# Three depthwise-conv tiles recast as half-length filters summed by accumulating transfers, and later weight remainders moved to VectorE

## The chip, the cores and the metric

The kernel runs on one core of one Trainium2 chip. The metric is device time of the whole program in microseconds (us), as the median of several runs. Five engines work beside each other: TensorE (PE, matmuls), VectorE (DVE), ScalarE (ACT), GpSimd (POOL) and SyncE (SP, which here only issues transfers). Each of them takes its instructions strictly in the order of the program and waits at the head of its queue for whatever that instruction needs.

## What is computed

One decoder layer over 1024 tokens with 1024 channels. The part that matters here is the conv group, 1024 channels in 8 tiles of 128, with a causal depthwise convolution of 31 taps:

```python
u = h @ w_in[l]
cv, cg, cs, lx, ls = jnp.split(u, [D_CONV, 2*D_CONV, 3*D_CONV, 3*D_CONV + D_LRU], axis=-1)
v = cv * jax.nn.sigmoid(cg)
v = causal_depthwise_conv(v, dw_w[l], dw_b[l])          # 31 taps
v = jax.nn.silu(layernorm(v, cln_g[l], cln_b[l]))       # over all 1024 channels
v = v @ pw2_w[l] + pw2_b[l]
y_conv = v * jax.nn.silu(cs)
...                                                     # lru group: short conv, two gates, linear scan
y = jnp.concatenate([y_conv, y_lru], axis=-1) @ w_out[l]
x = x + (1.0 + gate[:, None, :]) * y
```

An RMSNorm with a modulation computed from `c` comes before, another RMSNorm after.

## The kernel before

**Layout.** Channels lie on the 128 partitions, tokens along the free dimension; one activation tile is 128x1024 f32. There are 47 such buffers in SBUF (`big`). PSUM holds three 128x1024 tiles (`mm`) and one more (`acc`). Every f32 matmul is made of three products of rounded parts: high x high, high x low, low x high. So each weight tile is loaded by SP (`raw`), rounded on ACT (`whi`, L416) and its remainder is taken by a subtraction (`wlo`, `SUB`, L417). `weights()` (L427) does this for one tile; its default engine for the remainder is POOL. `raw`, `whi` and `wlo` have two buffers each.

**Slots.** PE's work goes in slots of 48 matmuls: 4 input tiles first (`FIRST`), 2 (`NEXT`), then the other input tiles mixed with the 8 pairs of lru gates, then 8 tiles of the lru half of the output, then the pointwise matmul and the rest of the output in pairs. `number[s]` numbers the weight tiles in that order: `NEXT` has 4 and 5.

**Order.** `Plan` is a list scheduler that runs at build time. Each operation has an engine, an estimated cost and a priority; `order()` plays them against a clock, takes the ready operation of smallest priority number on each free engine, and writes the program in that order. Conv work has priority number 1000 and up (L887), which fills what the other work leaves; the slots' own work has their number. `lock` marks operations that the planner keeps from running beside each other on DVE and POOL. The order is fixed once built: if an operation comes later on the chip than planned, all behind it on its engine comes later.

**The conv, `conv_tile(i)` (L886).** Six tiles go on DVE. The values are stored with the even tokens in the left half and the odd ones in the right (`apart`/`by_two`, L864 to L868; written by L974 and L1078). With `ev` and `od` those halves, three filters of half length are run over 512 tokens each: the even taps over `ev`, the summed taps over `ev+od`, the odd taps over `od`; 15 + 15 + 14 fused multiply-adds (L924, L926, L931) on accumulators in the PSUM tile `acc`, and three additions or subtractions put the result together. Tiles 2 and 5 (`POOLED`, L46) are done instead as 31 full-length products on ACT (`cq`, L894, L898), added one by one on POOL (L900).

**Around it.** `conv_sum()` (L940) sums the eight tiles in the order `SUMS` (L53), on POOL but for the last. `layer_norm()` (L1037) needs that sum; its mean and its 1/std are spread over the partitions by PE into `acc` tiles (L1039, L1054). `gate_mod()` (L1028) takes the modulation's gate in 8 pieces, one in each slot from `GM` = 22: a product on POOL and its sum on ACT (L715, L716). `gw_load()` (L949) takes the remainders of the gate weights on POOL.

Of the kernel before, what the change touches and what calls it, by code (L numbers as in the profile page):

```python
# [9 lines left out]
F32 = mybir.dt.float32  # L10
# [35 lines left out]
POOLED = (2, 5)  # L46
# [6 lines left out]
SUMS = (0, 1, 3, 2, 4, 6, 5, 7)  # L53
QRES = 4
GM = 22
# [22 lines left out]
class Op:  # L78
    __slots__ = ("eng", "cost", "emit", "prio", "table", "bufs", "succ", "wait", "ready",
                 "seq", "reserve", "columns", "lock", "end", "psum")  # L80


class Plan:
# [7 lines left out]
    def __init__(self, pools):  # L91
        self.pools = pools
        self.ops, self.writer, self.readers = [], {}, {}
# [13 lines left out]
    def op(self, eng, cost, emit, prio, r=(), w=(), table=None, after=(), reserve=0,  # L107
           columns=0, lock=False):
        o = Op()
        o.eng, o.cost, o.emit, o.prio, o.table = eng, cost, emit, prio, table  # L110
        o.succ, o.ready, o.seq, o.reserve = [], 0.0, len(self.ops), reserve
        o.columns = columns
        o.lock = eng == "POOL" or eng == "DVE" and lock
# [24 lines left out]

    def order(self):
# [19 lines left out]
        def done(o, end):  # L159
            o.end = until[o.eng] = end  # L160
            for b, w in o.psum:
                (b.written if w else b.read)[o.eng] = end
            for b in o.bufs:
                b.left -= 1
                if b.left == 0 and b.pool in free:
                    heapq.heappush(releases, (end, b.name, b.pool))
            for s in o.succ:
                lat = 0.0 if o.eng == "PE" and s.eng == "PE" else \
                    0.11 if o.eng == s.eng == "DVE" else self.LATENCY[o.eng]
                s.ready = max(s.ready, end + lat)  # L170
                s.wait -= 1
                if s.wait == 0:
                    pending[s.eng].append(s)

        while left:
# [3 lines left out]
            for e in engines:  # L179
# [42 lines left out]
                if e == "POOL" and held["DVE"] > t + 1e-9:  # L222
                    waiting, until[e] = o, float("inf")
                    continue
# [24 lines left out]
def hymba_layer(ctx: ExitStack, tc: tile.TileContext, xT, c_row, vecs, mod_w, w_first, w_in,  # L249
# [11 lines left out]
    psacc = ctx.enter_context(tc.tile_pool(name="psacc", bufs=1, space=bass.MemoryType.PSUM))  # L261
# [8 lines left out]
    pools["acc"] = (psacc, "acc", [P, T], 1)  # L270
# [46 lines left out]
    def TT(prio, eng, out, a, b, op, n=T, r=(), w=(), reserve=0, after=()):  # L317
        e = dve if eng == "DVE" else pool
        return S.op(eng, d_cost(n) if eng == "DVE" else p_cost(n),
                    lambda: e.tensor_tensor(out=out(), in0=a(), in1=b(), op=op), prio, r, w,  # L320
                    reserve=reserve, lock=not in_psum(r), after=after)

# [129 lines left out]
    def mm_tile(name, parts=2):  # L452
        return S.buf("mm", name, F32, parts)

    def acc_tile(name, parts=2):
        return S.buf("acc", name, F32, parts)
# [187 lines left out]
    psf = [mm_tile(f"first{n}", 4) for n in range(3)] + [acc_tile("first3", 4)]  # L644
    psb = psf[3]
# [15 lines left out]
    def fw_mm(prio, ps, i, xh, xl, k, cols, after=()):  # L661
        _, wh, wl = fw[k - k % 2]

        def emit():
            for lhs, rhs, last in ((wh, xh, 0), (wh, xl, 0), (wl, xh, 1)):
                for a, b in cols:
                    pe.matmul(ps()[:, a:b], fw_part(lhs, k, i * P, i * P + P)(),  # L667
                              rhs()[:, a:b], start=k == 0 and lhs is wh and rhs is xh,
                              stop=k == KT - 1 and bool(last), skip_group_check=True)
# [90 lines left out]
    st, wk = ctile("st", KT), halves(psb, H, T)  # L760

    def stats(sq, k):
        for b in range(KT):
            pe.matmul(psb()[:, H + b:H + b + 1], sq()[:, b * P:b * P + P], ones[:, 0:1],
                      start=k == 0 and b == 0, stop=k == len(sqs) - 1, skip_group_check=True)

    def spread_mm(a, e):
        for b in range(a // P, e // P):
            o = H + b * P - a
# [4 lines left out]
    ACT(RSP, lambda: st, lambda: psb()[:, H:H + KT], AF.Sqrt, KT, bias=eps_t, scale=1.0 / D,  # L774
        r=wk, w=[("st", 0)])
    S.op("DVE", 0.12, lambda: dve.reciprocal(st, st), RSP, [("st", 0)], [("st", 0)])
    for a, e in START:
        spread = S.op("PE", 0.22 * ((e - a) // P), lambda a=a, e=e: spread_mm(a, e), RSP,
                      [("st", 0)], wk, columns=4 * (e - a))
        ACT(RSP, part(rbc, a, e), part(psb, H, H + e - a), "copy", e - a, r=wk,  # L780
# [104 lines left out]

    def conv_tile(i):  # L886
# [6 lines left out]
        if i in POOLED:  # L893
            ACT(pr, ci, vi, AF.Identity, scale=w(0), bias=vec("dw_b", i), r=[vi, ("V", 1)],  # L894
                w=[ci])
            for s in range(1, TAPS):
                q = big_buf(f"cq{i}_{s}")
                ACT(pr, part(q, s, T), part(vi, 0, T - s), AF.Copy, T - s, scale=w(s), r=[vi],  # L898
                    w=[q], reserve=QRES)
                TT(pr, "POOL", part(ci, s, T), part(ci, s, T), part(q, s, T), ALU.add, T - s,  # L900
                   r=[ci, q], w=[ci])
            c[i] = ci
            return


        acc, b2 = acc_tile(f"cacc{i}"), bias2[:, i:i + 1]
        acc_e, acc_s, src_s = half(acc, 0), half(acc, 1), half(ci, 0)
# [8 lines left out]
        def every(o):  # L916
            return lambda: ci().rearrange("p (m q) -> p q m", q=2)[:, o]
        TT(pr, "DVE", src_s, ev, od, ALU.add, H, r=[vi], w=[(ci, 0)])
        ACT(pr, acc_e, ev, AF.Identity, H, scale=w(0), bias=vec("dw_b", i), r=[vi, ("V", 1)],
            w=[(acc, 0)])  # L920
        ACT(pr, acc_s, src_s, AF.Identity, H, scale=ws(0), bias=b2,
            r=[(ci, 0), ("V", 1), ("wsum", 0)], w=[(acc, 1)])
        for r in range(1, 16):
            STT(pr, cut(acc_e, r, H), cut(ev, 0, H - r), w(2 * r), cut(acc_e, r, H), ALU.mult,  # L924
                ALU.add, H - r, r=[vi, (acc, 0)], w=[(acc, 0)])
            STT(pr, cut(acc_s, r, H), cut(src_s, 0, H - r), ws(r), cut(acc_s, r, H), ALU.mult,  # L926
                ALU.add, H - r, r=[(ci, 0), (acc, 1)], w=[(acc, 1)])
        ACT(pr, every(1), acc_s, "copy", H, r=[(acc, 1)], w=[ci])
        ACT(pr, acc_s, od, AF.Copy, H, scale=w(1), r=[vi], w=[(acc, 1)])
        for r in range(1, 15):  # L930
            STT(pr, cut(acc_s, r, H), cut(od, 0, H - r), w(2 * r + 1), cut(acc_s, r, H), ALU.mult,  # L931
                ALU.add, H - r, r=[vi, (acc, 1)], w=[(acc, 1)])
        ACT(pr, every(0), acc_e, "copy", H, r=[(acc, 0)], w=[ci])
        TT(pr, "DVE", every(1), every(1), acc_e, ALU.subtract, H, r=[ci, (acc, 0)], w=[ci])
        TT(pr, "DVE", every(1), every(1), acc_s, ALU.subtract, H, r=[ci, (acc, 1)], w=[ci])
        TT(pr, "DVE", cut(every(0), 1, H), cut(every(0), 1, H), cut(acc_s, 0, H - 1), ALU.add,
           H - 1, r=[ci, (acc, 1)], w=[ci])
# [23 lines left out]
    def evac_in(m, ps, n, b=None, rb=()):  # L961
# [5 lines left out]
        elif kind == CV:  # L967
            sg = sig.pop(i)
            if i in POOLED:
                v[i] = sg  # L970
                TT(pr, "DVE", sg, ps, sg, ALU.mult, r=[ps, sg], w=[sg])
            else:
                v[i] = big_buf(f"v{i}")
                TT(pr, "DVE", apart(v[i], 0, T), by_two(ps, 0, T), by_two(sg, 0, T), ALU.mult,  # L974
                   r=[ps, sg], w=[v[i]])
# [61 lines left out]
    def layer_norm():  # L1037
        pr = 45
        mean = acc_tile("mean")  # L1039
# [14 lines left out]
        bc = acc_tile("lnbc")  # L1054
# [7 lines left out]
    for i, (s, ps) in enumerate(zip(FIRST, psf)):  # L1062
        j, p, bi = s[1] % KT, EVP + i, bias[:, i:i + 1]
        t = big_buf(f"first_u{i}", parts=4)
        for a, e in START:
# [4 lines left out]
            else:  # L1070
                for k in range(KT):
                    fw_mm(RSP + 60 + 0.1 * k, ps, i, uhs[k], uls[k], k, ((a, e),), after=[spread])
                TT(p, "DVE", part(t, a, e), part(ps, a, e), part(rbc, a, e), ALU.mult, n,
                   r=pk + halves(rbc, a, e), w=tk)
# [230 lines left out]
```

## Time and profile before

| | |
|---|---|
| median of 3 runs | 770.67 us (769.59 to 775.23) |
| profiled execution, its own time | 771.28 us |
| its span, first to last instruction | 769.4 us |
| granted TensorE clock, mean | 0.985 of full speed |
| transfers | 77.84 MB, all issued by SP |

The page gives each engine's busy time as a share of the span. A group of instructions is named by line, engine and `out<-in`; two figures behind the bar are its busy time in total and the mean length of one, and what follows is the time that the engine stood idle before them and who ended it. A row of a table of stretches gives for each engine busy us and the number of instructions, then the granted clock, the DMA share and GB/s. PE's matmuls overlap, so the length of one (some 390 ns) is longer than the distance from one to the next.

### The profile page before, as it was taken

Reading aid. Unit: us, or ns where it says so; the run is one execution under the profiler, and the core shown is the slowest. Engines: PE = TensorE matmul, PEld = TensorE weight load, DVE = VectorE, ACT = ScalarE, POOL = GpSimd, SP = SyncE. Lnnn points to the kernel's source line nnn. Section 1 sums busy time; section 2 is a strip of 40 time slices with the busy share of each in tenths; the row PEclk is TensorE's granted clock in tenths of the full one; section 3 lists DMA queues with packets and bytes.
Section 4 is the critical chain, followed back from the end, with each engine's and each line's share of the span. In section 5 each row is a group of like instructions: output and inputs, shape, how many; then the busy total and the mean of one; then the engine's idle time right before and its main releaser. Section 6 shows DMA issues by size and latency. Waiting matters only on the chain.

```text
span 769.4 us, 8629 instructions
## 1 busy us (share of the span) xinstructions
PE 733.5 (95%) x3288; PEld 606.0 (79%) x3288; DVE 665.6 (87%) x806; ACT 420.3 (55%) x473; POOL 323.1 (42%) x132
## 2 busy tenths in 40 slices
PE   3999899999999997999999998999999999999995
PEld 2888677888888885888888787788888888887885
DVE  7999999789899889999897998995977666999565
ACT  6630926997626477955956565664723223455220
POOL 0030312799899469989999612121220000000000
PEclk9999999999999999899999999999999999999997
DMA  9930221102102312331111012433332621425114
GB/s 329 406 118 32 83 82 35 55 27 83 63 28 83 116 55 83 116 110 56 55 55 55 27 55 81 138 136 111 136 115 96 200 110 40 152 83 177 43 55 164
DMA packets 24954, 77.84 MB, mean 101 GB/s; under 512 B 2768, under 2 KB 6096, under 8 KB 24912
## 3 DMA queue, kind: packets, MB, share of 16 engines
q1 hardware_dynamic: 24912, 77.28, 28.5%
q8 instruction: 26, 0.43, 0.2%
q14 instruction: 16, 0.13, 0.1%
HBM read 64.68 MB, written 12.58 MB: 100 GB/s over the span
## 4 chain that ended last, share of the span: by engine, by line
PE 57%; DVE 29%; ACT 7%; POOL 3%; issue 2%; DMA 1%; SPq 0%; DVEq 0%; ACTq 0%; POOLq 0%
PE ps L438 32%; DVE cacc L312 11%; PE first L667 6%; PE papw L559 5%; PE pbpw L559 4%; PE out L605 3%; ACT cq L301 3%; PE paout L559 2%; DVE r L1020 2%; PE pbout L559 2%; DVE xs L312 1%; DVE xs L320 1%; DVE yl L320 1%; DVE sls L320 1%; POOL c L320 1%
## 5 line engine op out<-in xcount | busy, mean ns | idle before, releaser
L320 POOL TENSOR_TENSOR wlo<-raw,whi 128x1024 fp32r<-128x1024 f32 x44 | 115.1, 2615 | 234.5 <-ACT whi L293 234.5
L438 PE MATMUL ps<-uh,whi 128*128 128x512 f32 x576 | 180.5, 395 | 7.0 <-ACT scs L301 6.6
L438 PE MATMUL ps<-ul,whi 128*128 128x512 f32 x576 | 179.7, 393 | 3.6 <-DVE ul L312 3.6
L438 PE MATMUL ps<-uh,wlo 128*128 128x512 f32 x576 | 179.3, 393 | 1.6 <-POOL wlo L320 1.6
L320 POOL TENSOR_TENSOR c<-c,cq 128x1023 f32<-128x1023 f32 (+29 forms) x60 | 159.8, 2663 | 9.5 <-ACT cq L301 7.0
L312 DVE SCALAR_TENSOR_TENSOR cacc<-v,V,cacc 128x511 f32<-128x511 f32 (+14 forms) x174 | 129.6, 745 | 13.7 <-ACT c L293 6.3
L438 PEld LDWEIGHTS ps<-uh,whi 128*128 128x128 f32 x576 | 109.4, 191 | 31.4 <-ACT scs L301 7.5
L438 PEld LDWEIGHTS ps<-ul,whi 128*128 128x128 f32 x576 | 109.3, 190 | 27.7 <-DVE ul L312 4.7
L438 PEld LDWEIGHTS ps<-uh,wlo 128*128 128x128 f32 x576 | 109.2, 190 | 24.8 <-POOL wlo L320 2.0
L293 ACT CAST whi<-raw 128x1024 fp32r<-128x1024 f32 x48 | 50.3, 1047 | 59.6 <-issue 34.4
L301 ACT ACTIVATE cq<-sig,V 128x1023 f32<-128x1023 f32 (+29 forms) x60 | 63.9, 1128 | 1.6 <-POOL c L320 1.6
L312 DVE SCALAR_TENSOR_TENSOR cacc<-c,wsum,cacc 128x511 f32<-128x511 f32 (+6 forms) x84 | 62.7, 746 | 2.3
L301 ACT ACT_TABLE_LOAD x45 | 57.7, 1283 | 1.6 <-PEq L1297 0.7
L438 PE MATMUL ps<-yh,whi 128*128 128x512 f32 x128 | 39.6, 391 | 0.0
L438 PE MATMUL ps<-yh,wlo 128*128 128x512 f32 x128 | 39.4, 389 | 0.0
L438 PE MATMUL ps<-yl,whi 128*128 128x512 f32 x128 | 39.4, 389 | 0.0
L667 PE MATMUL first<-uh,fhi 128*128 128x512 f32 x64 | 26.7, 416 | 11.1 <-ACT uh L301 11.1
L312 DVE SCALAR_TENSOR_TENSOR xs<-ps,V,xs 128x1023 f32<-128x1023 f32 (+2 forms) x24 | 30.6, 1274 | 2.6 <-ACT xs L301 2.5
L438 PEld LDWEIGHTS ps<-yl,whi 128*128 128x128 f32 x128 | 24.0, 188 | 5.0
L438 PEld LDWEIGHTS ps<-yh,wlo 128*128 128x128 f32 x128 | 24.0, 188 | 5.0
L667 PE MATMUL first<-ul,fhi 128*128 128x512 f32 x64 | 26.3, 411 | 1.7 <-DVE ul L312 1.7
L438 PEld LDWEIGHTS ps<-yh,whi 128*128 128x128 f32 x128 | 23.9, 188 | 4.9
(299 smaller groups left out, 1359.7 us busy)
## 6 DMA issues: line engine op xcount, KB each, us to landing
raw<-in_w_in_dram SPq DMA_DIRECT2D x36, 512.0 KB, 3.3
modw<-in_mod_w_dram SPq DMA_DIRECT2D x24, 512.0 KB, 7.8
raw<-in_w_out_dram SPq DMA_DIRECT2D x12, 512.0 KB, 3.9
scsd<-scs SPq DMA_DIRECT2D x8, 512.0 KB, 2.6
acc<-in_xT_dram SPq DMA_DIRECT2D x8, 512.0 KB, 4.6
accd<-acc SPq DMA_DIRECT2D x8, 512.0 KB, 2.8
rawpw<-in_pw_dram SPq DMA_DIRECT2D x8, 512.0 KB, 3.8
scsr<-scsd SPq DMA_DIRECT2D x8, 512.0 KB, 5.3
```

The source lines that it names most:

```text
L293: act.copy(out(), in_())
L301: act.activation(out=out(), in_=in_(), func=func, **kw)
L312: dve.scalar_tensor_tensor(out=out(), in0=in0(), scalar=scalar, in1=in1(), op0=op0, op1=op1, accum_out=accum)
L320: lambda: e.tensor_tensor(out=out(), in0=a(), in1=b(), op=op), prio, r, w,
L438: pe.matmul(ps()[:, a - off:b - off], k3(lhs)()[:, k, :], rhs[k]()[:, a:b], start=(k == 0 and lhs is wh and rhs is xh and (a - off) % H == 0),
L559: pe.matmul(half(*ps)(), half(*lhs)()[:, j * P:j * P + P], half(*rhs)(), start=start and j == 0 and z == 0, stop=j == KT // 2 - 1 and z == ...
L605: pe.matmul(ps()[:, a - off:e - off], k3(lhs)()[:, k, :], rhs()[:, i * H + a % H:i * H + a % H + e - a], start=k == KORD[0] and lhs is wh ...
L667: pe.matmul(ps()[:, a:b], fw_part(lhs, k, i * P, i * P + P)(), rhs()[:, a:b], start=k == 0 and lhs is wh and rhs is xh, stop=k == KT - 1 a ...
L1020: S.op("DVE", 2.2, lambda: dve.tensor_tensor_scan(out=r(), data0=a(), data1=xs(), initial=0.0, op0=ALU.mult, op1=ALU.add), pr, [a, xs], [r])
```

## The change

It has four parts.

1. `POOLED` becomes (2, 4, 5). These three tiles get the half-length form as well, in `conv_pooled`: ACT makes products of 512 tokens, two of them (even-tap and summed-tap filter) side by side in one 128x1024 buffer, and a transfer issued by POOL adds that buffer to the accumulator `es` in SBUF; pairs of odd-tap products go to `oo` in the same way. 22 such transfers for one tile. Four DVE operations and two ACT copies put the result together. No POOL arithmetic is left in these tiles, and each v is stored apart, as for the other tiles.
2. `weights()` takes the remainder on POOL only for tiles numbered under `EARLY` = 10, later ones on DVE.
3. The PSUM tile `acc` becomes two half tiles of 128x512. The two accumulators of a DVE conv tile are held apart; `first3`, the token statistics and the late half of the fourth first tile get one each; the mean and 1/std of the layer norm go into `mm` tiles.
4. `apart` and `by_two` keep the same places, but walk all even tokens and then all odd ones, instead of pairs. `SUMS` becomes (0, 1, 3, 2, 6, 4, 7, 5). In the DVE conv tiles the copy of `acc_e` and its subtraction come ahead of the odd filter.

The planner's model of an accumulating transfer is: `ISSUE` = 1.0 us on POOL, then landed `FLIGHT` = 7.0 us later, and not less than `RATE` = 3.0 us after the one before.

```diff
-POOLED = (2, 5)
+POOLED = (2, 4, 5)
-SUMS = (0, 1, 3, 2, 4, 6, 5, 7)
+SUMS = (0, 1, 3, 2, 6, 4, 7, 5)
+AHEAD = 3
+FOLD = "DVE"
+EARLY = 10
+ISSUE, FLIGHT, RATE = 1.0, 7.0, 3.0
...
-            o.end = until[o.eng] = end
+            until[o.eng] = end
+            if o.lag:
+                self.adder = max(self.adder + o.lag, end + FLIGHT)
+                end = self.adder
+            o.end = end
...
-    pools["acc"] = (psacc, "acc", [P, T], 1)
+    pools["acc"] = (psacc, "acc", [P, H], 2)
...
+    def ADD(prio, out, a, n=T, r=(), w=(), after=()):
+        return S.op("POOL", ISSUE, lambda: pool.dma_start(out(), a(), accum_op=ALU.add), prio, r,
+                    w, lag=RATE * n / T, after=after)
...
-    def weights(s, after=(), n=None, eng="POOL"):
+    def weights(s, after=(), n=None, eng=None):
         n = number[s] if n is None else n
+        eng = eng or ("POOL" if n < EARLY else "DVE")
...
     def by_two(b, a, e):
-        return lambda: b()[:, a:e].rearrange("p (m q) -> p m q", q=2)
+        return lambda: b()[:, a:e].rearrange("p (m q) -> p q m", q=2)
     def apart(b, a, e):
-        return lambda: b().rearrange("p (q m) -> p m q", q=2)[:, a // 2:e // 2]
+        return lambda: b().rearrange("p (q m) -> p q m", q=2)[:, :, a // 2:e // 2]
...
+    def conv_pooled(i, pr, ci, vi, src, wts, every):
+        (ev, src_s, od), (w, ws) = src, wts
+        def two(b, r):
+            return lambda: b().rearrange("p (z m) -> p z m", z=2)[:, :, r:]
+        es, oo, adds = big_buf(f"es{i}", parts=2), big_buf(f"oo{i}", parts=2), []
+        def product(to, z, r, x, key, scale, bias=None):
+            ACT(pr, part(to, z * H + r, z * H + H), lambda: x()[:, :H - r],
+                AF.Copy if bias is None else AF.Identity, H - r, bias=bias, scale=scale,
+                r=[key, ("V", 1), ("wsum", 0)], w=[(to, z)],
+                after=adds[-AHEAD:][:len(adds) // AHEAD][:1])
+        for r in range(16):
+            q = es if r == 0 else big_buf(f"cq{i}_{r}", parts=2)
+            product(q, 0, r, ev, vi, w(2 * r), None if r else vec("dw_b", i))
+            product(q, 1, r, src_s, (ci, 0), ws(r), None if r else bias2[:, i:i + 1])
+            if r:
+                adds.append(ADD(pr, two(es, r), two(q, r), r=[es, q], w=[es]))
+            if r % 2:
+                continue
+            q = oo if r == 0 else big_buf(f"co{i}_{r}", parts=2)
+            product(q, 0, r, od, vi, w(2 * r + 1))
+            if r < 14:
+                product(q, 1, r, od, vi, w(2 * r + 3))
+            if r == 14:
+                adds.append(ADD(pr, part(oo, r, H), part(q, r, H), H, r=[(oo, 0), (q, 0)],
+                                w=[(oo, 0)]))
+            elif r:
+                adds.append(ADD(pr, two(oo, r), two(q, r), r=[oo, q], w=[oo]))
+        ACT(pr, every(1), half(es, 1), "copy", H, r=[es], w=[ci])
+        ACT(pr, every(0), half(es, 0), "copy", H, r=[es], w=[ci])
...
+        TT(pr, FOLD, part(oo, 1, H), part(oo, 1, H), part(oo, H, T - 1), ALU.add, H - 1, r=[oo],
+           w=[oo])
+        last(FOLD, 1, 0, H, es, 0, ALU.subtract)
+        last(FOLD, 1, 0, H, oo, 0, ALU.subtract)
+        last(FOLD, 0, 1, H, oo, 0, ALU.add)
...
-        mean = acc_tile("mean")
+        mean = mm_tile("mean")
-        bc = acc_tile("lnbc")
+        bc = mm_tile("lnbc")
```

More of the change, by code (lines that the diff above doesn't have):

```diff
@@ L112, in op @@
         o.columns = columns
-        o.lock = eng == "POOL" or eng == "DVE" and lock
+        o.lock = not lag and eng == "POOL" or eng == "DVE" and lock
         r, w = list(self.keys(r)), list(self.keys(w))
@@ L221, in order @@
                         free[b.pool] -= 1
-                if e == "POOL" and held["DVE"] > t + 1e-9:
+                if e == "POOL" and o.lock and held["DVE"] > t + 1e-9:
                     waiting, until[e] = o, float("inf")
@@ L779, in hymba_layer @@
                       [("st", 0)], wk, columns=4 * (e - a))
-        ACT(RSP, part(rbc, a, e), part(psb, H, H + e - a), "copy", e - a, r=wk,
+        ACT(RSP, part(rbc, a, e), part(psb, 0, e - a), "copy", e - a, r=wk,
             w=halves(rbc, a, e))
@@ L892, in conv_tile @@
         ci, vi = big_buf(f"c{i}", parts=2), v[i]
[L893 to L907, printed above, removed]
+        b2, src_s = bias2[:, i:i + 1], half(ci, 0)
         ev, od = (lambda: vi()[:, :H]), (lambda: vi()[:, H:])
@@ L918, in conv_tile @@
         TT(pr, "DVE", src_s, ev, od, ALU.add, H, r=[vi], w=[(ci, 0)])
+        if i in POOLED:
+            conv_pooled(i, pr, ci, vi, (ev, src_s, od), (w, ws), every)
+            return
+        acc, acs = acc_tile(f"cacc{i}"), acc_tile(f"caccs{i}")
+        acc_e, acc_s = half(acc, 0), half(acs, 0)
         ACT(pr, acc_e, ev, AF.Identity, H, scale=w(0), bias=vec("dw_b", i), r=[vi, ("V", 1)],
-            w=[(acc, 0)])
-        ACT(pr, acc_s, src_s, AF.Identity, H, scale=ws(0), bias=b2,
-            r=[(ci, 0), ("V", 1), ("wsum", 0)], w=[(acc, 1)])
+            w=[acc], after=held[-1:])
@@ L931, in conv_tile @@
             STT(pr, cut(acc_s, r, H), cut(od, 0, H - r), w(2 * r + 1), cut(acc_s, r, H), ALU.mult,
[L932 to L935, printed above, removed]
+                ALU.add, H - r, r=[vi, acs], w=[acs])
+        TT(pr, "DVE", every(1), every(1), acc_s, ALU.subtract, H, r=[ci, acs], w=[ci])
```

67 lines of the change are left out of this document (38 added, 29 removed).

## The prediction

> **What bounds the kernel now.** I read the page's busy times first, then a table of stretches, then who PE waited for.
>
> ```profile
> span 769.4 us, 8629 instructions
> PE 733.5 (95%) x3288; PEld 606.0 (79%) x3288; DVE 665.6 (87%) x806; ACT 420.3 (55%) x473; POOL 323.1 (42%) x132
> ```
>
> PE is busy for 95% and its 3288 matmuls aren't touched, so no more can be won than PE's losses: its idle time, 769.4 - 733.5 = 35.9 us, and what it lost at a lower clock. The stretches show where:
>
> ```profile
> core 0: us, PE busy (x) PEld busy (x) DVE busy (x) ACT busy (x) POOL busy (x), PEclk, DMA share, GB/s
> 0.00:20.00 20.00, 7.22 (x17) 5.34 (x18) 14.55 (x46) 13.33 (x18) 0.70 (x6) 1.00 0.91 331
> 80.00:100.00 20.00, 16.42 (x72) 12.84 (x71) 20.00 (x24) 17.25 (x23) 7.63 (x2) 0.95 0.30 100
> 100.00:120.00 20.00, 19.64 (x84) 15.88 (x84) 19.48 (x27) 8.00 (x8) 4.81 (x2) 0.97 0.11 41
> 280.00:300.00 20.00, 18.42 (x82) 14.91 (x81) 16.97 (x21) 18.33 (x22) 20.00 (x9) 1.00 0.18 63
> 300.00:320.00 20.00, 15.81 (x60) 12.54 (x59) 17.77 (x22) 16.18 (x20) 19.84 (x9) 0.83 0.28 105
> 340.00:360.00 20.00, 20.00 (x90) 16.57 (x89) 19.47 (x23) 14.00 (x18) 17.80 (x8) 1.00 0.11 36
> 470.00:480.00 10.00, 7.59 (x27) 5.85 (x26) 7.61 (x12) 5.97 (x7) 2.17 (x1) 0.84 0.24 79
> 740.00:769.40 29.40, 20.58 (x152) 19.48 (x150) 18.18 (x38) 4.31 (x10) 0.00 (x0) 0.84 0.40 144
> ```
>
> An undisturbed stretch (340:360) holds 90 matmuls in 20 us, one per 0.222 us. Counting matmuls takes idle time and lost clock together. Missing are 18 + 6 in 80:120 (5.3 us), 8 + 30 in 280:320 (8.4 us, with the clock granted at 0.83) and 45 - 27 = 18 in 470:480 (4.0 us, clock 0.84). These 17.7 us lie where conv work runs. The first 20 us are loads and the last 29 the final norm; the change doesn't reach either.
>
> ```profile
> PE ps L438 <- ACT scs L301: 6.6, 2, 4.2
> PE ps L438 <- DVE ul L312: 3.6, 2, 3.4
> PE ps L438 <- POOL wlo L320: 1.6, 1, 1.6
> ACT modw L301 <- POOL modw L320: 15.5, 5, 7.2
> ACT c L293 <- DVE cacc L312: 17.1, 3, 7.0
> ```
>
> PE waits for ACT to empty a PSUM tile (scs); ACT itself hung on something late. For 280:320 ACT's timeline names it:
>
> ```profile
> 297.37 1.03 ACT L301 ACTIVATE sls<-ps 128x1024 f32<-128x1024 f32 x1
> 303.53 1.06 ACT L301 ACTIVATE modw<-modw 128x1024 f32<-128x1024 f32 x1 [5.14 <-POOL modw L320]
> 306.88 1.01 ACT L301 ACTIVATE scs<-ps 128x1024 f32<-128x1024 f32 x1
> ```
>
> POOL was busy for 20.00 of 20 us, so its modulation product came late, ACT stood behind it for 5.14 us, and scs behind that. At 470 the copy c held ACT until DVE's filter was done (the 7.0 us wait). Both are lateness against a fixed order, and the groups show whence:
>
> ```profile
> L320 POOL TENSOR_TENSOR c<-c,cq 128x1023 f32<-128x1023 f32 (+29 forms) x60 | 159.8, 2663 | 9.5 <-ACT cq L301 7.0
> L320 POOL TENSOR_TENSOR wlo<-raw,whi 128x1024 fp32r<-128x1024 f32 x44 | 115.1, 2615 | 234.5 <-ACT whi L293 234.5
> L320 DVE TENSOR_TENSOR sls<-sls,r 128x1024 f32<-128x1024 f32 x8 | 19.1, 2384 | 0.0
> L320 DVE TENSOR_TENSOR xs<-xs,r 128x1024 f32<-128x1024 f32 x8 | 17.1, 2143 | 0.0
> L320 DVE TENSOR_TENSOR xsl<-xs,xsh 128x1024 fp32r<-128x1024 f32 x8 | 16.0, 2004 | 0.0
> L320 DVE TENSOR_TENSOR wlo<-raw,whi 128x1024 fp32r<-128x1024 f32 x4 | 4.9, 1216 | 0.0
> ```
>
> The same DVE operation on two SBUF operands takes 1.216 us where POOL is idle (wlo, near the end) and 2.0 to 2.4 us while POOL works. In these three groups alone, 52.2 - 24 x 1.216 = 23.0 us of DVE are lost to POOL.
>
> **The change part by part.**
>
> ```profile
> L312 DVE SCALAR_TENSOR_TENSOR cacc<-v,V,cacc 128x511 f32<-128x511 f32 (+14 forms) x174 | 129.6, 745 | 13.7 <-ACT c L293 6.3
> L301 ACT ACTIVATE cq<-sig,V 128x1023 f32<-128x1023 f32 (+29 forms) x60 | 63.9, 1128 | 1.6 <-POOL c L320 1.6
> L301 ACT ACTIVATE cacc<-v,V 128x512 f32<-128x512 f32 x12 | 8.7, 728 | 6.8 <-DVE c L320 6.7
> L320 DVE TENSOR_TENSOR c<-c,cacc 128x512 f32<-128x512 f32 x12 | 8.3, 688 | 0.4
> L293 ACT COPY c<-cacc 128x512 f32<-128x512 f32 x12 | 7.4, 616 | 17.2 <-DVE cacc L312 17.1
> ```
>
> POOL loses 159.8 us of additions and 38 of 44 remainders (`NEXT` and numbers 6 to 9 stay), 38 x 2.615 = 99.4 us. It gains 66 transfer issues. POOL issues none before; by its other rows one takes between 0.3 us (the planner allows 1.0) and the 2.4 us of a full addition, 20 to 158 us. It is relieved either way.
>
> DVE gains 38 x 1.216 = 46.2 us of remainders, 12 closing operations x 0.688 = 8.3 us and two sums for tiles 2 and 5, 1.4 us. It loses tile 4: 44 multiply-adds x 0.745 + 3 x 0.688 = 34.8 us. Net +21.1 us, against at least the 23.0 us of stretching that POOL caused and now mostly cannot. DVE comes out level or lighter.
>
> ACT: tiles 2 and 5 go from 31 x 1.128 = 35.0 us each to 47 half products x 0.728 + 2 x 0.616 = 35.4 us, nothing. Tile 4 adds 35.4 less its old three products and two copies, 3.4: 32.0 us. ACT goes from 55% to 59%. What hides this is its idle time; if ACT is late anyway, each us of it stands before a PSUM evacuation.
>
> The walk over the halves: where `v` is written pairwise it takes 2.044 us against 1.214 us for the plain product.
>
> ```profile
> L320 DVE TENSOR_TENSOR v<-ps,sig 128x1024 f32<-128x1024 f32 x4 | 8.2, 2044 | 0.0
> L320 DVE TENSOR_TENSOR sig<-ps,sig 128x1024 f32<-128x1024 f32 x2 | 2.4, 1214 | 0.0
> L312 DVE SCALAR_TENSOR_TENSOR v<-first_u,bias,first_u 128x512 f32<-128x512 f32 x4 | 6.6, 1686 | 0.0
> ```
>
> Between nothing and 0.83 us each is won; I take most of it, since the strided `c<-c,cacc` above shows no such price (0.688 us for 512). The four `v<-first_u` lie in front of the `ul` that PE awaits at 80:100; (1.686 - 0.745) x 4 = 3.8 us at most, part of it stretching by a POOL remainder that stays. I take 1.3 of the 5.3 us there.
>
> Layer norm: mean and 1/std now hold one of three `mm` tiles, the mean for as long as the eight `c<-c,mean` last (row below, 501.2 to 513.7). Two tiles still alternate, 10.7 us (48 x 0.222) per slot, and a slot's tile is emptied by one DVE operation. I take nothing; what hides it is DVE's slack in that stage, and were DVE nearly a slot late, it would be one stall like that at 470, 4.0 us.
>
> The transfers are the unknown. Within a tile, 15 additions into `es` form a chain: POOL issues one only when the one before has landed. Behind a waiting issue on POOL stand the gate weights' remainders, the modulation products (for which ACT waits) and csum. On ACT, a product waits for the addition three back, and behind it stand the casts `whi` and the evacuations for which PE waits. On DVE the closing operations wait for the last one.
>
> ```profile
> scsd<-scs SPq DMA_DIRECT2D x8, 512.0 KB, 2.6
> raw<-in_w_in_dram SPq DMA_DIRECT2D x36, 512.0 KB, 3.3
> fraw<-in_w_first_dram SPq DMA_DIRECT2D x3, 512.0 KB, 10.2
> q1 hardware_dynamic: 24912, 77.28, 28.5%
> L301 ACT ACTIVATE c<-sig,V x2: 1245/1246/1246, 135.9 to 276.5; 128x1024 f32<-128x1024 f32 x2
> L320 POOL TENSOR_TENSOR c<-c,cq x60: 2329/2382/4346, 138.3 to 421.3; 128x1023 f32<-128x1023 f32 x2, 128x1022 f32<-128x1022 f32 x2, 128x1021 f32<-128x1021 f32 x2, 128x1020 f32<-128x1020 f32 x2
> L320 DVE TENSOR_TENSOR c<-c,mean x8: 1211/1212/1220, 501.2 to 512.5; 128x1024 f32<-128x1024 f32 x8
> ```
>
> 512 KB occupy the 16 transfer engines for 0.285 x 769.4 / 77.28 x 0.524 = 1.5 us. An addition reads its target as well: 3.0 us. From issue to landing, a bound from below is a store, 2.6 + 1.5 = 4.1; from above a load in the saturated start, 10.2 + 1.5 = 11.7. I take 4.8 (raw, 3.3 + 1.5), as the share of the transfer engines is 0.11 to 0.28 in the rows above, far from the 0.91 of the start. With 0.3 to 2.4 us of issue a step of the chain takes 5.1 to 7.2 us. The planner allows 1.0 + 7.0 + 0.15 = 8.15, so the additions would land ahead of plan and nothing would wait for them. Tile 5 is multiplied from 276.5 on; 15 x 8.15 = 122 us later it is 399, 100 us ahead of the mean at 501. The 66 additions take 66 x 3.0 = 198 us of transfer engines in these 363 us.
>
> The Trainium skill (DMA: Bandwidth & Descriptors, section on the anatomy of one DMA on the GpSimd path) gives a fixed 2.0 us plus bytes at 436 GB/s; by that an addition reading 1.05 MB is 4.4 us, an estimate, and no run here shows such a transfer yet.
>
> Sum, on the profiled execution's 771.28 us: 8.4 us go at 280:320 (the additions and remainders that filled POOL ahead of that modw have left it), 4.0 at 470 (DVE less stretched), 1.3 at 80:120: 13.7 us. The order is new as a whole, and the old one had two large stalls of its own; I put one of the size of that at 470, 4.0 us, against it. 771.28 - 13.7 + 4.0 = 761.6 us; the profiled run lies 0.6 above the median, so 761.0.
>
> **The rivals.**
>
> *Additions later than planned (slower).* The point is 8.15 us per step. POOL's additions reached from 2.329 to 4.346 us where DVE held them up; were the issue of a transfer held up likewise, by 2.0 us, a step would take 7.2 + 2.0 = 9.2 us, 1.05 over plan. The chains of tiles 2, 4 and 5 follow and overlap from 136 to 399 us, 263 / 8.15 = 32 steps; products that wait on them carry the lag into ACT and so into PE: 32 x 1.05 = 34 us. 771.3 - 13.7 + 34 - 0.6 = 791 us; with half the excess 774. Against it: the 4.8 us above. For it: the 5.14 us row shows ACT passing such lateness straight on to PE. The Trainium skill (SBUF — State Buffer, section on SBUF's two separate sides) knows this as a trap: transfers issued by GpSimd starve while DVE runs in a mode that takes both ports, and took 3.1 us instead of 0.62. The rows above agree that DVE and POOL hold each other up, but the page names copies, and DVE's rows here are two-input operations. 0.22.
>
> *The gain is given back (no change).* Remainders on DVE queue behind scans and filters, and DVE now stands still itself when a cast `whi` is late (POOL's 234.5 us of idle time was waiting for it). PE's 1.6 us for wlo shows that it runs close. Three stalls of 4.0 us: 771.3 - 13.7 + 12 - 0.6 = 769 us, 765 to 776. 0.25.
>
> *The change doesn't do what it says:* additions that POOL still makes, say, would leave 770; nothing in the diff speaks for it, 0.01.
>
> **How the numbers follow.** Forecast 0.52, with a range of its own from 753 (all 17.7 us, no new stall: 771.3 - 17.7 - 0.6) to 768. With the rivals the range goes from 752 to 788; beyond lie half of the slow rival, 0.11, and some 0.03 below. One per cent is 763.0 to 778.4, about what can be told from no change. Faster: 0.45 of the forecast's 0.52 counts. Within: 0.07 of it, 0.22 of the second rival, 0.01 of the third, 0.03 of the slow one make 0.33. Slower: 0.19 of the slow rival and 0.03 of the second, 0.22.
>
> **What would show it.** Right: POOL under 200 us busy, DVE's sls and xs groups near 1.2 us, no wait of PE on scs near 300 and 470, additions landing within 8 us of each other. Wrong: idle time of ACT before `cq`/`co` products or `modw` that ends with a transfer, PE waiting for DVE's wlo, a lowered clock in 140:420.

## The result and the profile after

| | before | after |
|---|---|---|
| median | 772.39 us (769.59 to 775.23, 4 runs) | 852.94 us (848.3 to 855.03, 4 runs) |
| ratio to before | | 1.1034, 95% interval 1.0969 to 1.11 |
| profiled execution, its span | 771.28 us, 769.4 us | 852.65 us, 850.4 us |

The changed kernel is 10.3% slower, outside the predicted range. The page after, with its span, the busy times and the queue that POOL's transfers use:

```profile
span 850.4 us, 8751 instructions
PE 750.8 (88%) x3288; PEld 615.1 (72%) x3288; DVE 621.9 (73%) x811; ACT 444.0 (52%) x553; POOL 139.5 (16%) x100
q0 software_dynamic: 17568, 33.30, 23.5%
```

Every other engine is less busy than PE, DVE and POOL less than before, and still PE stands idle for 850.4 - 750.8 = 99.6 us against 35.9. Nothing is overloaded on this page. A table of stretches shows where the time goes (columns as in the prediction's tables: PE, PEld, DVE, ACT, POOL, granted clock, DMA share, GB/s), first after, then two stretches of before:

```profile
80.00:120.00 40.00, 37.58 (x160) 29.68 (x159) 39.53 (x53) 26.48 (x32) 12.58 (x4) 0.96 0.23 75
120.00:260.00 140.00, 140.00 (x619) 116.04 (x618) 121.50 (x150) 97.08 (x120) 32.69 (x26) 1.00 0.63 132
260.00:520.00 260.00, 188.23 (x744) 149.09 (x743) 123.16 (x138) 137.95 (x186) 83.51 (x59) 0.86 0.67 137
520.00:820.00 300.00, 296.48 (x1309) 244.40 (x1310) 246.16 (x287) 141.51 (x156) 2.40 (x1) 0.99 0.31 108
```

```profile
260.00:500.00 240.00, 231.45 (x997) 189.26 (x996) 223.90 (x219) 160.71 (x172) 174.75 (x66) 0.98 0.22 75
500.00:740.00 240.00, 238.22 (x1068) 196.79 (x1066) 184.64 (x217) 100.14 (x115) 16.84 (x7) 1.00 0.32 112
```

From 120 to 260 PE is busy without a gap, at the full clock, and does 619 matmuls in 140 us, one per 0.226 us. (The prediction's 0.222 us was read from 20 us.) At that rate 260 us hold 1150. After, 744 were done between 260 and 520: 406 are missing, 91.8 us. Before, 240 us hold 1061 and 997 were done: 64 missing, 14.5 us. The difference, 77 of the 81.0 us between the spans, lies in this one stretch, which is where the tiles 4 and 5 are convolved. DVE, which was full there, is busy for 123.16 of 260 us, so it is being kept waiting too.

Who waits for whom (columns: engine, its tile and line, the releaser, us in total, times, longest):

```profile
ACT modw L310 <- POOL modw L329: 50.5, 6, 13.8
POOL es L334 <- issue: 99.1, 23, 8.0
POOL oo L334 <- issue: 40.6, 10, 4.7
PE ps L453 <- ACT scs L310: 20.4, 2, 10.2
PE gate L1060 <- ACT sls L310: 17.3, 2, 12.5
PE ps L453 <- ACT whi L302: 13.6, 3, 6.3
PE gate L1060 <- ACT xsh L302: 13.5, 2, 10.9
```

Read from the bottom: PE waits for ACT, for evacuations and casts; ACT waits for POOL's modulation product, 50.5 us where it was 15.5; and POOL waits for nothing that the profile can name. "Issue" is time in which no semaphore was outstanding. It stands ahead of POOL's transfer issues. One such chain, in three timelines (start, length, engine, operation, idle time before it), POOL, ACT, PE:

```profile
306.93 1.21 POOL L334 DMA_DIRECT2D es<-cq  x1 [4.62 <-issue]
312.27 1.20 POOL L334 DMA_DIRECT2D oo<-co  x1 [4.12 <-issue]
317.58 1.21 POOL L334 DMA_DIRECT2D oo<-co  x1 [4.11 <-issue]
318.33 2.83 POOL L329 TENSOR_TENSOR modw<-modw,sc 128x1024 f32<-128x1024 f32 x1
```

```profile
321.20 1.06 ACT L310 ACTIVATE modw<-modw 128x1024 f32<-128x1024 f32 x1 [13.83 <-POOL modw L329]
326.00 1.02 ACT L310 ACTIVATE sls<-ps 128x1024 f32<-128x1024 f32 x1
```

```profile
327.07 1.22 PE L1060 MATMUL gate<-xsh,ghi 128*128 128x512 f32 x2 [12.53 <-ACT sls L310]
```

Three additions begin 5.34 and 5.31 us apart, although the first goes into `es` and the second into `oo` and neither needs the other. The modulation product stands behind them on POOL and begins 0.75 us after the third; ACT has stood for 13.83 us for it, `sls` comes behind that, and PE has stood for 12.53 us for `sls`. From issue to landing an addition took this long (the tile `es`):

```profile
DMA to landing us min/median/max: 5.0/5.2/8.9
```

So the next full addition is issued about when the one before has landed, whatever it adds to. A smaller one isn't held up in that way. The last odd-tap product of a tile has half the size, 249 KB, and goes right behind a full one, 0.72 us after it:

```profile
473.17 1.21 POOL L334 DMA_DIRECT2D es<-cq  x1 [4.14 <-issue]
473.89 1.43 POOL L334 DMA_DIRECT2D oo<-co  x1
```

That pointed to room for transfers in flight. Both kernels are built with this line (L1297 before, L1351 after), which no part of the change touches; its last argument is called the scratch below:

```python
nc = _bacc.Bacc("TRN2", target_bir_lowering=False, num_devices=1, dynamic_dma_scratch_size=1024)
```

Before, POOL issued no transfer, and the size couldn't matter. The Trainium skill (DMA: Bandwidth & Descriptors, section on SWDGE, HWDGE and iDMA) says that GpSimd writes the descriptors of its transfers, the orders that the transfer engines carry out, into rings in a part of SBUF set aside for them, from which the transfer engines drain them; that section gives no size at which this becomes a limit. The two theories were then: the scratch is the cause, or the order (a lag that any addition slower than `RATE` = 3.0 us causes).

### The profile page after: what moved, and what is told of

Its sections match the earlier page's. It is cut to its first block, busy times and chain, and to the rows that moved or that the text cites. A ratio compares the mean times of both kernels' runs of the same rounds, so it can differ in the third digit from the quotient of the medians.

```text
span 850.4 us, 8751 instructions
## 1 busy us (share of the span) xinstructions
PE 750.8 (88%) x3288; PEld 615.1 (72%) x3288; DVE 621.9 (73%) x811; ACT 444.0 (52%) x553; POOL 139.5 (16%) x100
## 5 line engine op out<-in xcount | busy, mean ns | idle before, releaser
L329 DVE TENSOR_TENSOR wlo<-raw,whi 128x1024 fp32r<-128x1024 f32 x42 | 52.7, 1254 | 49.9 <-ACT whi L302 49.9
L334 POOL DMA_DIRECT2D es<-cq x45 | 54.6, 1214 | 190.9 <-issue 99.1
L321 DVE SCALAR_TENSOR_TENSOR caccs<-v,V,caccs 128x511 f32<-128x511 f32 (+6 forms) x70 | 52.0, 743 | 7.0 <-ACT caccs L310 6.2
L321 DVE SCALAR_TENSOR_TENSOR cacc<-v,V,cacc 128x511 f32<-128x511 f32 (+14 forms) x75 | 55.6, 741 | 0.2
L321 DVE SCALAR_TENSOR_TENSOR caccs<-c,wsum,caccs 128x511 f32<-128x511 f32 (+6 forms) x70 | 52.1, 744 | 0.8
L310 ACT ACTIVATE cq<-v,V 128x511 f32<-128x511 f32 (+14 forms) x45 | 31.6, 706 | 17.2 <-DMA es<-cq 15.6
L1060 PE MATMUL gate<-xsh,ghi 128*128 128x512 f32 x32 | 12.7, 483 | 30.7 <-ACT sls L310 17.3
L334 POOL DMA_DIRECT2D oo<-co x21 | 26.6, 1268 | 78.8 <-issue 40.6
L321 DVE SCALAR_TENSOR_TENSOR r<-a,r 128x1024 f32<-128x1024 f32 x8 | 10.4, 1306 | 33.9 <-ACT r L310 33.9
L310 ACT ACTIVATE modw<-modw 128x1024 f32<-128x1024 f32 x8 | 8.4, 1054 | 50.5 <-POOL modw L329 50.5
```

Of the source, the lines that this page charges most:

```text
L310: act.activation(out=out(), in_=in_(), func=func, **kw)
L321: dve.scalar_tensor_tensor(out=out(), in0=in0(), scalar=scalar, in1=in1(), op0=op0, op1=op1, accum_out=accum)
L334: return S.op("POOL", ISSUE, lambda: pool.dma_start(out(), a(), accum_op=ALU.add), prio, r, w, lag=RATE * n / T, after=after)
L1060: pe.matmul(ps()[:, c0:c1], lhs()[:, j, :], rhs()[:, c0:c1], start=st == 0, stop=st == 2)
```

## The experiments

The first four ran on one chip beside the kernel before (770.24 us), the next four likewise (769.74), the last four again (770.54). Ratios are to that time, with 95% intervals.

### Twice the scratch, same order

```diff
-    small = ctx.enter_context(tc.tile_pool(name="small", bufs=4))
+    small = ctx.enter_context(tc.tile_pool(name="small", bufs=3))
...
-    ones = const.tile([P, P], F32, tag="ones", name="ones")
+    ones = const.tile([P, 1], F32, tag="ones", name="ones")
...
-    ones_d = const.tile([P, P], F32, tag="ones_d", name="ones_d")
+    ones_d = const.tile([P, 1], F32, tag="ones_d", name="ones_d")
...
-                pe.matmul(mean()[:, a:b], ones_d, csum()[:, a:b], start=True, stop=True)
+                pe.matmul(mean()[:, a:b], ones_d.to_broadcast([P, P]), csum()[:, a:b], start=True, stop=True)
...
-    nc = _bacc.Bacc("TRN2", target_bir_lowering=False, num_devices=1, dynamic_dma_scratch_size=1024)
+    nc = _bacc.Bacc("TRN2", target_bir_lowering=False, num_devices=1, dynamic_dma_scratch_size=2048)
```

The small tiles make room in SBUF; each engine's instructions stand in the same order as in the changed kernel.

> The changed kernel with the scratch that holds the descriptors of POOL's transfers doubled to 2048 bytes per partition, every engine's order of instructions as in the changed kernel. Theory (scratch): the old scratch holds the descriptors of one full addition, so POOL cannot write the next until the first has drained; with twice the room, additions to different accumulators start 1.2 to 3.5 us apart instead of 5.3, POOL's idle time before es and oo falls from 270 us to under 100, the lag is gone and the time is 755 to 790 us. Rival (one at a time): transfers from POOL are served one after the other whatever the room; spacing stays at 5.3 us and the time at 845 to 860. Rival (remainders): the loss comes from the weight remainders on VectorE; the spacing may fall, the time stays above 830.

Measured: 772.0 us, 1.002 (1.000 to 1.004); 81 us less than the changed kernel. POOL's two groups of transfers (busy us and mean ns, then idle time ahead of them and its releasers), first after, then with the larger scratch:

```profile
L334 POOL DMA_DIRECT2D es<-cq x45 | 54.6, 1214 | 190.9 <-issue 99.1
L334 POOL DMA_DIRECT2D oo<-co x21 | 26.6, 1268 | 78.8 <-issue 40.6
```

```profile
L334 POOL DMA_DIRECT2D es<-cq x45 | 59.7, 1345 | 77.6 <-ACT cq L310 32.7
L334 POOL DMA_DIRECT2D oo<-co x21 | 26.0, 1258 | 65.7 <-ACT co L310 63.4
```

POOL's idle time ahead of the two groups fell from 269.7 to 143.3 us, not to under 100 as expected, but what POOL waits for now has a name, ACT's products. Additions follow each other closely, three within 1.5 us (POOL's timeline), and land later (the tile `es`):

```profile
300.14 2.44 POOL L334 DMA_DIRECT2D oo<-co  x2
301.62 2.20 POOL L334 DMA_DIRECT2D es<-cq  x1
```

```profile
DMA to landing us min/median/max: 5.0/7.3/13.5
```

The scratch is the cause of nearly all of the loss. That descriptors of one full addition fill more than half of 1024 is inferred from the 5.3 us and the 0.72 us; the ring itself isn't in the trace. But the kernel is then only level with the one before. The stretch 260 to 400, before, after, and with the larger scratch:

```profile
260.00:400.00 140.00, 134.23 (x581) 110.26 (x580) 131.31 (x131) 99.92 (x115) 128.13 (x49) 0.98 0.22 77
```

```profile
260.00:400.00 140.00, 100.19 (x393) 79.59 (x393) 56.63 (x60) 75.23 (x109) 50.78 (x34) 0.85 0.70 152
```

```profile
260.00:400.00 140.00, 127.82 (x547) 104.53 (x546) 90.76 (x94) 106.26 (x149) 66.68 (x49) 0.96 0.97 200
```

547 matmuls, where this stretch without a gap holds 620 (the eighth run, below): 73 x 0.226 = 16 us are still lost, and the transfer engines are now busy for 0.97 of the time. 36 of the 66 additions begin in these 140 us; at 3.0 us each they make a share of 0.77, and the rest of the kernel's transfers had 0.22 there before. One stall can be followed to a transfer that came late (POOL, ACT, then PE's wait, whose longest is this one):

```profile
297.86 2.34 POOL L329 TENSOR_TENSOR modw<-modw,sc 128x1024 f32<-128x1024 f32 x1 [6.61 <-DMA modw<-in_mod_w_dram]
300.23 1.06 ACT L310 ACTIVATE modw<-modw 128x1024 f32<-128x1024 f32 x1 [5.85 <-POOL modw L329]
PE ps L453 <- ACT scs L310: 11.3, 2, 7.1
```

In this stretch the loads of modulation weights took up to 10.5 us to land, against 4.4 before.

### The planner told the truth

```diff
-ISSUE, FLIGHT, RATE = 1.0, 7.0, 3.0
+ISSUE, FLIGHT, RATE = 1.2, 4.2, 5.35
```

> The changed kernel with the planner told what the trace shows (1.2 us of issue, landed 4.2 us later, one addition per 5.35 us); scratch as in the changed kernel. Theory (lag against a fixed order): the loss is ScalarE and POOL standing at the head of their queues behind additions that the order placed too early; an order made for 5.35 us brings most of it back, 770 to 800 us, with the additions still 5.3 us apart and ending near 500 us. Rival (capacity): 66 additions of 5.35 us are 353 us and simply too much whatever the order; the layer norm comes as late as now and the time stays above 835.

843.2 us, 1.096 (1.0908 to 1.1011), where the rival had it. The order now allows for the spacing, and the time hardly falls. In this order the additions come further apart than they need, one per (585.1 - 133.4) / 65 = 6.9 us, the last at 585.1, 71 us later than in the changed kernel, and POOL still stands for 80.1 us ahead of the `es` additions with "issue" as the reason. A lag against a plan that didn't know of the spacing is therefore not the whole of it; three tiles at this spacing cost time in this planner's order too. Whether another order would do better isn't shown.

### Two tiles by transfers, small scratch

```diff
-POOLED = (2, 4, 5)
+POOLED = (2, 5)
...
-SUMS = (0, 1, 3, 2, 6, 4, 7, 5)
+SUMS = (0, 1, 3, 2, 4, 6, 7, 5)
```

> The changed kernel with tiles 2 and 5 alone by accumulating transfers, tile 4 back on VectorE as the other tiles. 44 additions instead of 66. Theory (lag): the planned 3.0 us per addition is still wrong, but tile 2 is over before tile 5 begins and the backlog stays within one tile; 785 to 815 us. Rival (remainders): VectorE carries 35 us more than in the changed kernel on top of the remainders, so the time rises, above 855.

761.78 us, 0.9903 (0.987 to 0.9935), faster than before and better than either theory had it. How much room the additions had is read from the row of the `es` additions (number, length, first and last start), after, with the larger scratch, and here:

```profile
L334 POOL DMA_DIRECT2D es<-cq x45: 1186/1215/1229, 145.4 to 514.1; - x45
```

```profile
L334 POOL DMA_DIRECT2D es<-cq x45: 1187/1206/2203, 143.5 to 432.1; - x45
```

```profile
L334 POOL DMA_DIRECT2D es<-cq x30: 1200/1216/1229, 145.0 to 425.0; - x30
```

With room for more, all 66 additions came between 134.0 and 432.1 us, one per 298 / 65 = 4.6 us: closer than 5.3. Here the 44 come between 135.1 and 425.0, one per 6.7 us: wider than 5.3, and the limit bites less. (The first addition of each run goes into `oo`.)

### All of the change but the transfers

```diff
+        if i in POOLED:
+            ACT(pr, ci, vi, AF.Identity, scale=w(0), bias=vec("dw_b", i), r=[vi, ("V", 1)],
+                w=[ci])
+            for s in range(1, TAPS):
+                q = big_buf(f"cq{i}_{s}")
+                ACT(pr, part(q, s, T), part(vi, 0, T - s), AF.Copy, T - s, scale=w(s), r=[vi],
+                    w=[q], reserve=QRES)
+                TT(pr, "POOL", part(ci, s, T), part(ci, s, T), part(q, s, T), ALU.add, T - s,
+                   r=[ci, q], w=[ci])
+            c[i] = ci
+            return
```

with `POOLED` = (2, 5) and the old `SUMS`: tiles 2 and 5 as before the change, tile 4 on DVE, later remainders on DVE, half tiles, new walk.

> Everything of the change but the accumulating transfers: tiles 2 and 5 by ScalarE products and POOL additions as before, tile 4 on VectorE; later weight remainders on VectorE, two half accumulators, the walk over the halves and the layer norm's tiles as changed. Theory (the transfers alone are the loss): 760 to 778 us, near the kernel before, VectorE fuller by the remainders (46 us) less what POOL no longer stretches. Rival (remainders): the remainders on VectorE are the loss, 800 us or more, with TensorE waiting for wlo.

767.44 us, 0.9954 (0.9932 to 0.9975), within the theory's range: the later remainders on DVE are not the loss. Without a transfer the other parts win 2.8 us. With transfers for two tiles (the run above, same chip) it is 5.7 us more.

### Both: two tiles and twice the scratch

The edits of the first and the third experiment together.

> Tiles 2 and 5 alone by transfers (as in e3, 761.8 us) with the doubled scratch of e1. Theory (scratch): the 5.3 us between additions that still hold POOL in e3 go, and with 44 additions the transfer engines stay under the 0.9 to 1.0 share that e1 had in 260:400; 752 to 760 us. Rival (chain): with two tiles that hardly overlap, each addition waits for the one before in its own chain, which the scratch doesn't shorten; no difference from e3, 760 to 764.

759.36 us, 0.985 (0.9819 to 0.9881). Within the theory's range, near the rival's: with two tiles the scratch is worth little.

### The modulation products off POOL

```diff
-        dot("POOL", n, 2 * KT + j)
+        dot("DVE", n, 2 * KT + j)
```

in the changed kernel. If ACT's wait for `modw` is the cost, it goes.

> The changed kernel (old scratch) with the eight modulation products of gate_mod taken off POOL: one VectorE multiply with its sum each, no ScalarE sum. Theory (POOL's queue in front of ScalarE): of ScalarE's waits in the changed kernel the largest is the 50.5 us for modw behind additions, and it is what TensorE waits for at 300:340; without it 800 to 825 us. Rival (capacity): ScalarE's products wait for the additions anyway and the additions end no sooner; the wait moves to other instructions and the time stays above 838.

851.67 us, 1.1058 (1.1005 to 1.1111): no gain. The 50.5 us of waiting are gone, and PE waits as long for others of ACT's operations:

```profile
PE gate L1060 <- ACT xsh L302: 23.8, 4, 11.1
PE ps L453 <- ACT scs L310: 20.2, 2, 10.4
PE gate L1060 <- DVE xsl L329: 13.7, 3, 8.2
```

`modw` was where the lag passed from POOL to ACT, not its cause; ACT's `cq` products now stand for 29.6 us until an `es` addition has landed, where it was 15.6.

### Products further ahead of the additions

```diff
-AHEAD = 3
+AHEAD = 8
```

> The changed kernel (old scratch) with AHEAD = 8 for 3, so that a product waits for the addition eight back. Theory (POOL's queue): ScalarE's waits on transfers, some 50 us, shrink, those for modw stay; 825 to 850 us. Rival (ScalarE's own waits are the loss): under 810 us.

856.67 us, 1.1113 (1.1063 to 1.1164), above both expectations. The wait of ACT's `cq` products for `es` additions didn't shrink, as the theory had it; it grew from 15.6 to 38.9 us. Whether they then wait for the eighth addition back or for a free buffer wasn't followed. The last addition starts at 527.2 us, 13 us later.

### Two tiles, twice the scratch, modulation on DVE

> As e5, with the modulation products on VectorE as in e6. With the scratch no longer in the way, POOL's queue should be short and the products early: no difference from e5 within 4 us (theory), since VectorE takes on 8 x 1.36 = 11 us. Rival: modw behind additions still holds ScalarE, and 5 us or more are won over e5.

755.21 us, 0.9789 (0.9759 to 0.982): the best of all, 2.1% faster than before. Against the fifth run on the same chip, 4.15 us are won, a little more than the theory's 4 us of no difference. The stretch 260 to 400:

```profile
260.00:400.00 140.00, 140.00 (x620) 115.91 (x618) 137.58 (x179) 87.43 (x110) 32.84 (x24) 1.00 0.65 149
```

PE is busy without a gap where before it lost most, at the full clock; the transfer engines are at 0.65.

### Three tiles, twice the scratch, modulation on DVE

> Three tiles by transfers with the doubled scratch (e1, 772.0 us) and the modulation products on VectorE. Open is why e1 wins nothing although the additions no longer hold each other up. Theory (transfer engines full): in e1 their share is 0.9 to 1.0 over 260:400, additions land after 7.3 us and more, modulation weights arrive late; moving the products takes no byte off, so the products wait elsewhere: 766 to 773 us. Rival (POOL's queue): the modulation products behind additions hold ScalarE as in the kernel before; 755 to 763 us.

773.37 us, 1.0036 (1.0024 to 1.0047), 0.4 us above the theory's range and far from the rival's.

```profile
260.00:400.00 140.00, 127.22 (x542) 103.99 (x541) 100.36 (x120) 100.69 (x136) 54.36 (x42) 0.95 0.98 204
```

The edit that helped with two tiles does nothing with three. DVE's products now stand for 19.8 us until modulation weights have landed, where it is 1.2 us with two tiles (the eighth run). Transfer engines at 0.98 of the time are the likely next limit; this stretch and the one of the first experiment agree on it, though no run changed the transfers' load there by itself.

### The modulation on DVE without transfers

The same edit of `dot` in the kernel before, and in the fourth experiment's kernel.

> The kernel before with the modulation products on VectorE and nothing else. In its profile 8.4 us were lost at 280:320 where ScalarE stood behind such a product. Theory: POOL's full queue in front of ScalarE was that loss, 760 to 765 us. Rival (VectorE is at 92% and more in that stage): what is won is lost again to VectorE, 767 to 773 us.

> As e4 (no accumulating transfers, remainders on VectorE, 767.4 us) with the modulation products on VectorE. It tells whether the transfers earn anything in e8 (755.2 us). Theory (the transfers free POOL and VectorE of each other): without them 760 us or more. Rival (the products' place alone makes e8): 753 to 758 us.

783.26 us, 1.0165 (1.015 to 1.0181), and 787.57 us, 1.0212 (1.0192 to 1.0232). Both are slower, the first against both expectations, the second as the theory had it (760 or more). In the kernel before with that edit, DVE's products and its shared work:

```profile
L312 DVE SCALAR_TENSOR_TENSOR modw<-modw,sc 128x1024 f32<-128x1024 f32 x24 | 37.6, 1574 | 1.9 <-DMA modw<-in_mod_w_dram 1.9
L320 DVE TENSOR_TENSOR sls<-sls,r 128x1024 f32<-128x1024 f32 x8 | 16.0, 2006 | 0.0
```

So the gain of the eighth run isn't that edit's alone: beside the transfers of two tiles it helps, without transfers it costs 1.7% and (from 0.9954) 2.6%. The 1.574 us is a mean over 24 products, 16 of which ran before 65 us in either kernel; the eight that were moved took 2.006 us each (16.0 us between 250 and 420), against 1.223 us in the eighth run, and `sls` still takes 2.0, as POOL goes on adding. But each run has a new order throughout, and what part of the loss is DVE's load and what the order's wasn't told apart.

### The best version with all remainders back on POOL

```diff
-EARLY = 10
+EARLY = 99
```

> As e8 with all remainders of the input weights back on POOL, beside the additions' issues. Theory (POOL has room once the scratch is large enough, and VectorE gains 46 us): within 4 us of e8's 755.2. Rival (remainders queue behind issues that wait for a chain): TensorE waits for wlo, 762 us or more.

766.23 us, 0.9937 (0.9919 to 0.9954), some 11 us slower than the best by the two ratios ((0.9937 - 0.9789) x 770). The same DVE group with remainders on DVE, and on POOL:

```profile
L329 DVE TENSOR_TENSOR xs<-xs,r 128x1024 f32<-128x1024 f32 x8 | 9.8, 1220 | 0.1
```

```profile
L329 DVE TENSOR_TENSOR xs<-xs,r 128x1024 f32<-128x1024 f32 x8 | 16.4, 2046 | 0.1
```

Part 2 of the change is a gain here, and POOL's arithmetic stretches DVE's. The time is the rival's (762 or more), but not by its way: PE never waits for `wlo` in this run. It loses most between 400 and 520, 501 matmuls for 540 in the best version, 8.8 us; how the longer DVE operations bring that about wasn't followed.

## Why the prediction was wrong

**The step that failed** is the one on transfers: "The 66 additions take 66 x 3.0 = 198 us of transfer engines in these 363 us", and with it the test of a chain step against 8.15 us, "so the additions would land ahead of plan and nothing would wait for them". With twice the scratch, and the order unchanged, 81 us of the time go. The 3.0 us is right as a load on the engines (0.235 x 850.4 / 66 = 3.03 us), and so is the step, predicted 5.1 to 7.2 us, measured 5.2 in the median. Wrong was to take additions to different accumulators as free to overlap. POOL issues them one per 5.3 us at the closest, and with more room the same order had them one per 4.6 in the mean. I compared the latency of a chain with the plan's 8.15, and the throughput with the transfer engines' share; the throughput of the issuing engine, against the planner's own `RATE` of 3.0 us, I didn't compare at all. 65 x (5.3 - 4.6) = 46 us of lag follow at once; that the last addition came 514.1 - 432.1 = 82 us later has more in it, since POOL's products stand between the additions, and ACT, held up itself, delivers late. That remainder wasn't split further.

**What bounds the kernel** was right: PE's losses decide, and they changed in the stretch named. 260 to 500 held the loss before and holds it after.

**POOL relieved**: right by the page, 323.1 to 139.5 us, and 66 issues of 54.6 + 26.6 = 81.2 us, inside 20 to 158. It misled all the same: an engine busy for 16% was the one that set the pace.

**DVE level or lighter**: right, 665.6 to 621.9 us. The groups after:

```profile
L329 DVE TENSOR_TENSOR sls<-sls,r 128x1024 f32<-128x1024 f32 x8 | 12.7, 1588 | 0.0
L329 DVE TENSOR_TENSOR xs<-xs,r 128x1024 f32<-128x1024 f32 x8 | 9.8, 1220 | 0.1
L329 DVE TENSOR_TENSOR v<-ps,sig 128x1024 f32<-128x1024 f32 x6 | 7.3, 1220 | 3.7 <-DMA es<-cq 3.7
L321 DVE SCALAR_TENSOR_TENSOR v<-first_u,bias,first_u 128x512 f32<-128x512 f32 x4 | 5.0, 1278 | 0.0
```

`xs` fell from 2.143 to 1.220 us, `sls` only to 1.588; products and sums are left on POOL, and with the products gone from it too (the eighth run) `sls` takes 1.220. The walk over halves won all of its 0.83 us on `v`. In 80:120, taken as one stretch, PE did 160 matmuls instead of 155: 1.1 us won, 1.3 taken.

**ACT** rose by 23.7 us, 444.0 - 420.3, less than the 32.0 predicted. It is busy for 52%; its idle time was spent waiting.

**The forecast's gain** of 13.7 - 4.0 us is about what the change brings with two tiles, 8.5 us at the old scratch and 10.4 with the larger one, though that is another kernel than the one forecast. With three tiles it doesn't come even so: the larger scratch gives 772.0 us, with the transfer engines busy for 0.97 of 260:400. The check of 198 us against 363 averaged over a stretch in which the additions aren't spread evenly (25 began in 120:260, 36 in 260:400), and left out the kernel's other transfers.

**The slow rival** had the sign and the way: POOL, `modw`, ACT, PE. It put the cause into each addition (9.2 us per step, measured 5.2) and the price at 34 us for 81. The 45 issues into `es` took 1.186 to 1.229 us while DVE worked. The trap that the Trainium skill names (SBUF — State Buffer, section on SBUF's two separate sides), issues starved by DVE, is therefore not seen here.

**The rival of the gain given back** expected DVE's remainders to hold things up. PE did wait for them, 4.8 us where it had waited 1.6 for POOL's, but in the best version they win 11 us.

**What would show it**: all three signs given for "wrong" came: a lowered clock in 140:420 (0.85 in 260:400), idle time of ACT ahead of the `cq` products that ended with a transfer (15.6 us by the table of waits), and PE waiting for DVE's `wlo` (4.8 us). The signs for "right" that came, POOL under 200 us, `xs` near 1.2 us and additions landing within 8 us (median 5.2, the longest 8.9), say nothing of how far apart the additions start.

**Left open**: a scratch beyond 2048 with three tiles, and parts 3 and 4 of the change each by itself, weren't tried.

## What to carry to other kernels

Where an engine begins to issue transfers, ask how many can be in flight before asking how long one takes: the spacing of independent transfers, held against the rate at which the order wants them, sets the pace, and it may hang on a setting far from the change. The wait that the profile put down to "issue", on an engine with little to do, was a limit on resources here and not slack; it is worth a search. And of a bundle of edits, run the parts: two tiles instead of three, with the limit lifted, beat both kernels.

## What was not expected of the hardware

- With a scratch of 1024, full accumulating transfers (497 to 511 KB, 128 partitions) began no closer than 5.3 us behind one another, whatever they added to; with 2048 three began within 1.5 us, and the whole kernel fell from 852.94 to 772.0 us.
- One at a time, such an addition took 5.0 us at the least and 5.2 in the median from issue to landing, of which POOL is held for 1.2 us; with several in flight the median rose to 7.3 us and the longest to 13.5. The Trainium skill's fit (DMA: Bandwidth & Descriptors, section on the anatomy of one DMA on the GpSimd path) made it 4.4 us, an estimate; the measurement decides, 0.6 us or more longer.
- Scans on DVE were stretched too. With the remainders back on POOL (the last run) one took 3.164 us. Before, with POOL adding, and after:

```profile
L1020 DVE TENSOR_TENSOR_SCAN r<-a,xs 128x1024 f32<-128x1024 f32 x8 | 27.6, 3453 | 0.0
```

```profile
L1072 DVE TENSOR_TENSOR_SCAN r<-a,xs 128x1024 f32<-128x1024 f32 x8 | 18.3, 2285 | 0.1
```
